# A hybrid attention and convolution layer on one core: an input weight laid out piece by piece, its last piece in another buffer, and one partition sum for two

## The chip, the cores and the metric

One Trainium2 chip, one of its cores. The metric is the device time of one execution in microseconds (us), as a median of repeated runs. "PE" is TensorE, "DVE" VectorE, "ACT" ScalarE, "POOL" GpSimd, "SP" SyncE, which here only issues DMAs.

## The reference, cut to what matters

```python
h = rms_norm(x, pre_norm_gain)
q, k, v, z_a, b_gate, c_gate, u, z_c = split(h @ w_in, 8)
lam = exp(sum(lq1 * lk1)) - exp(sum(lq2 * lk2)) + lambda_init
attn = rms_norm(diff_attention(q, k, v, lam, slopes), subln_gain) * (1 - lambda_init) * silu(z_a)
y = b_gate * causal_conv3(c_gate * u) * silu(z_c)
x = x + rms_norm(concat(attn, y) @ w_out, post_norm_gain)
e = rms_norm(p @ w_ple_proj, ple_norm_gain)
out = x + sigmoid(x @ w_ple_gate) * e
```

x is 1024 positions by 1024 features, p 1024 by 256, all in fp32. The change touches the embedding branch, `e`: the product of p with `w_ple_proj`, and the root mean square over e's 1024 features, of which each position needs one.

## The kernel before, in words

Features lie on the partitions and positions in the free dimension. The 1024 positions are two halves of 512, n = 0 and 1, so a tile is 128 x 512. Every product of two fp32 operands is made of three matmuls in the type fp32r (`mm3`, L99 to L102) from operands split into a high and a low part (`split`, L87 to L93): ACT casts the high part (L89, or L92 with a scale), and DVE or POOL subtracts it from the source (L90, L93).

**Start** (L336 to L361). Nine matmuls on zeros, then `embed` (L322) makes e for half 0 and half 1: eight tiles of 128 features, m = 0 to 7, six matmuls each; each tile is copied by ACT or DVE (L330, L332) and stored to memory, `e_dram` (L333). Its weight `in_w_ple` is loaded in four pieces by `load_ple` (L300): tile 0, tile 1, tiles 2 and 3 with 37 columns of small constants behind them (549 columns), and tiles 4 to 7 (1024 columns). Each piece is split into `wph` and `wpo` (for tiles 0 and 1 by DVE alone, L308, L309; for the others by ACT and DVE, L311). In memory the whole weight is one array of 128 rows by 2085 columns, so that a piece is a band of columns of it. The pieces land in buffers `rawe` of the pool `rawp`, which has three; the fourth piece has to wait for one of them to be read. `load_p` (L313) loads p into `p_raw`, one of the three buffers of the pool `wp` that later hold split weights. `load_x` (L295) loads the 16 tiles of x, `mix`, on the same queue of SP, and splits each into `hT`. `wq` and `wk` (L359, L360) are the first projection's weights, cast by ACT (L89, `w<-raw`).

**Four heads** (L470 to L495). For each head the steps of `PLAN` (L31) are run: `a` softmax of query blocks (`Head.softmax`, L216: PE scores `s`, DVE row maximum and bias at L237, ACT exponential at L241, DVE combination of the two maps at L246 to L249), `g` the values (transposes `tpw` at L260, split by ACT and DVE into `wt`, product `av`), `n` its norm and scale (`scale_values`, L279), `c` tiles of the convolution branch (`Conv`, L410), whose projections `pj` fill PE, `z` the gate, `s` the sums of the embedding.

**Sums of the embedding**, `embed_scale` (L446), run for half 0 in head 0 and half 1 in head 1, behind the values' last instruction (L492). It reads the eight tiles of e again from `e_dram`, ACT squares them (L452) and POOL adds them up (L454), into `mix[7][n]`. `column_sums` (L105) then sums over the partitions: DVE transposes blocks of 32 x 32 (`flip`, L107), reduces them to 16 columns (`part`, L109), and one matmul with a constant, `fold`, (L116) makes the sum, `ms`. `rsqrt` (L95) is one DVE step and a power on POOL (L97, `small_c<-small_c` for the embedding), and L457 halves the result, which is kept in `rs_e`, 16 columns a half, until the last stage needs it. The same `column_sums` serves the heads' norms, with further columns.

**Output** (L498 to L594): the product with `w_out`, its norm, the product with the gate's weight, and the store.

The program's loops only record the work. The order of the instructions on every engine is set afterwards by the scheduler of the tile framework, from its own simulation (`schedule_with_timeline_sim=True`, L628). An engine runs its own list strictly in order. So a change of a few lines can move instructions far from them.

Of the kernel before, what the change touches and what calls it, by code (L numbers as in the profile page):

```python
# [30 lines left out]
PLAN = [  # L31
# [4 lines left out]
]  # L36

# [6 lines left out]
def hybrid_layer(ctx, tc, xT, pT, w_in, lams, w_out, w_ple, w_gate, outT):  # L44
# [11 lines left out]
    tiny = ctx.enter_context(tc.tile_pool(name="tiny", bufs=3))  # L56
    dram = ctx.enter_context(tc.tile_pool(name="dram", bufs=1, space=DRAM))

    small_c = edge.tile([P, 96], F32, name="small_c")
    ps_s = ctx.enter_context(tc.tile_pool(name="ps_s", bufs=3, space=PSUM))  # L60
    ps_a = ctx.enter_context(tc.tile_pool(name="ps_a", bufs=1, space=PSUM))

# [10 lines left out]
    make_identity(nc, ident)  # L73
    fold = const.tile([P, P], F32, name="fold")
    own = small_c[:, 0:4]
    nhalf = small_c[:, 4:20]
    G.memset(nhalf, -0.5)
    sm = small_c[:, 20:57]
    subg = small_c[:, 57:58]
# [22 lines left out]
        T.matmul(out=ps, lhsT=al, rhs=bh, start=False, stop=last)  # L102


    def column_sums(acc, pool, extra=None, tag="flip"):  # L105
        flip = pool.tile([P, HALF], F32, tag=tag, name="flip")
        V.transpose(out=flip, in_=acc)  # L107
        part = tiny.tile([P, 32], F32, tag="part", name="part")
        V.tensor_reduce(out=part[:, 0:16], in_=flip.rearrange("p (f r) -> p f r", r=32), axis=AX.X, op=add)  # L109
        if extra is not None:  # L110
            V.tensor_tensor(out=part[:, 16:32].rearrange("p (t f) -> p t f", t=4),
                            in0=extra.unsqueeze(2).broadcast_to([P, 4, 4]),
                            in1=own.unsqueeze(1).broadcast_to([P, 4, 4]), op=mult)
        n = 16 if extra is None else 32
        ms = bank_t("ms")
        T.matmul(out=ms[:, :n], lhsT=fold, rhs=part[:, :n], start=True, stop=True)  # L116
        return ms
# [37 lines left out]
    with ExitStack() as st:  # L155
# [130 lines left out]
        with ExitStack() as st0:  # L286
            sp = st0.enter_context(tc.tile_pool(name="sp", bufs=1))
            s2 = st0.enter_context(tc.tile_pool(name="s2", bufs=2))

            wph = sp.tile([P, KT, 2, P], F32R, name="wph")  # L290
            wpo = sp.tile([P, KT, 2, P], F32R, name="wpo")

            splits = {}

            def load_x(n, kts=range(KT)):  # L295
                for kt in kts:
                    nc.sync.dma_start(out=mix[kt][n], in_=xT[n, kt])
                    splits[n, kt] = split(hT[n][kt][:, 0], hT[n][kt][:, 1], mix[kt][n], col(C_PRE, kt))

            def load_ple(c, o, queue=nc.sync, constants=0):  # L300
                n = (c.stop - c.start) * 2 * P
                raw = rawp.tile([P, n + constants], F32, tag="raw", name="rawe")
                queue.dma_start(out=raw, in_=w_ple[:, o:o + n + constants])
                if constants:
                    V.tensor_copy(out=sm, in_=raw[:, n:])
                raw = raw[:, :n].rearrange("p (a b c) -> p a b c", b=2, c=P)
                if c.start < 2:
                    V.tensor_copy(out=wph[:, c], in_=raw)  # L308
                    V.tensor_tensor(out=wpo[:, c], in0=raw, in1=wph[:, c].bitcast(F32), op=sub)  # L309
                else:  # L310
                    split(wph[:, c], wpo[:, c], raw)  # L311

            def load_p(n):  # L313
                pth = s2.tile([P, 2, HALF], F32R, tag="pth", name="pth")
                pto = s2.tile([P, 2, HALF], F32R, tag="pto", name="pto")
                raw = p_raw[:, n].bitcast(F32).rearrange("p (k a) b -> p k (a b)", k=2)
                for k in range(2):
                    nc.sync.dma_start(out=raw[:, k], in_=pT[:, n, k])
                    last = split(pth[:, k], pto[:, k], raw[:, k])
                return pth, pto, last  # L320

            def embed(n, p):  # L322
                pth, pto, _ = p
                for m in range(KT):
                    ps = bank_s("ple") if m % 2 else bank_t("ple")
                    for k in range(2):
                        mm3(ps, wph[:, m, k], wpo[:, m, k], pth[:, k], pto[:, k], k == 0, k == 1)
                    e = s2.tile([P, HALF], F32, tag="e", bufs=5, name="e")
                    if m % 2:
                        A.copy(out=e, in_=ps)  # L330
                    else:
                        V.tensor_copy(out=e, in_=ps)  # L332
                    nc.sync.dma_start(out=e_dram[n, m], in_=e)  # L333


            zero = sp.tile([P, HALF], mybir.dt.bfloat16, name="zero")  # L336
            V.memset(zero, 0.0)
            idle = bank_p("idle")
            for _ in range(9):
                T.matmul(out=idle, lhsT=zero[:, :P], rhs=zero, start=True, stop=True)  # L340
            p_raw = wp.tile([P, 2, KT, P], F32R, tag="w", name="p_raw")
            load_ple(slice(0, 1), 0, nc.scalar)
            pt0 = load_p(0)
            load_ple(slice(1, 2), 256)
            load_ple(slice(2, 4), 512, constants=37)
            load_ple(slice(4, 8), 1024 + 37)
            with tc.issue_after(pt0[2][1].ins):
                for g in range(4):
                    V.tensor_reduce(out=fold[:, 32 * g:32 * g + 32], in_=ident.rearrange("p (a b) -> p b a", a=4),
                                    axis=AX.X, op=add)  # L350
                V.tensor_reduce(out=own, in_=ident.rearrange("p (f r) -> p f r", r=32), axis=AX.X, op=add)
            embed(0, pt0)
            V.tensor_scalar(out=subg, in0=sm[:, C_SUB:C_SUB + 1], scalar1=0.4, scalar2=None, op0=mult)
            load_x(0, range(4))
            pt1 = load_p(1)
            load_x(0, range(4, KT))
            embed(1, pt1)
            mixing_weight()
            wq = w_in_tile(0, 0, V)  # L359
            wk = w_in_tile(1, 0, V)  # L360
            load_x(1)  # L361
# [84 lines left out]
        def embed_scale(n):  # L446

            acc = mix[7][n]
            for m in range(KT):
# [2 lines left out]
                A.activation(out=e, in_=e, func=AF.Square)  # L452
                if m:
                    G.tensor_tensor(out=acc, in0=acc, in1=e, op=add)  # L454
            r = rs_e[:, 16 * n:16 * n + 16]
            rsqrt(r, column_sums(acc, ap)[:, :16], D, 1e-6)
            V.tensor_scalar(out=r, in0=r, scalar1=0.5, scalar2=None, op0=mult)  # L457

        convs = [Conv(ct) for ct in range(4)]
        fill = [(part, cv, ev) for cv in convs for part, ev in ((6, cv.ev_u), (5, cv.ev_c), (7, cv.ev_y), (4, cv.ev_b))]  # L460
# [9 lines left out]
        for h in range(H):  # L470
# [5 lines left out]
            for step in PLAN[h]:  # L476
# [8 lines left out]
                elif k == "g":  # L485
                    hd.values(int(v))
                elif k == "n":
                    hd.scale_values(int(v))
                elif k == "c":
                    conv_tiles(int(v))  # L490
                elif k == "s":
                    with tc.issue_after(hd.last.ins):  # L492
                        embed_scale(int(v))
                elif k == "t":
                    conv_tiles(int(v), together=True)  # L495

# [135 lines left out]
```

## Time and profile before

| | us |
|---|---|
| three runs | 639.99, 640.1, 641.1 |
| median | 640.1 |
| the profiled execution | 640.71 |
| its span on the core | 638.9 |
| PE busy | 631.2 (99% of the span) |
| DVE busy | 448.9 (70%) |
| ACT busy | 241.7 (38%) |
| POOL busy | 227.2 (36%) |

The span is the time from the first to the last recorded instruction; 1.8 us of the execution lie outside it. Busy time is the time in which an engine has an instruction in work. A PE that is busy for 99% of the span can only be made to end sooner by taking matmuls away, or by closing the few gaps between them. PE's matmuls overlap: a matmul of 512 columns is listed with about 0.39 us, but the next one starts 0.23 us behind it, so gaps are read from the starts.

### The profile page before, as it was taken

How to read it: one execution, taken by the hardware profiler on the slowest of the kernel's cores; microseconds unless marked ns; L12 is line 12 of the kernel's file. 1: busy time of each engine (PE TensorE's matmuls, PEld its weight loads, DVE VectorE, ACT ScalarE, POOL GpSimd, SP SyncE). 2: the span in 40 equal slices, each digit the busy share in tenths (PEclk: the TensorE clock that was granted, in tenths of full speed). 3: DMA queues.
4: the chain of work that ended last, by engine and by line, in shares of the span. 5: the costliest groups of instructions: out<-in, count | busy, mean ns of one | idle time of the engine just before them, and what ended most of it. 6: DMA issues, size and time to landing. Idle time of an engine off the chain costs nothing.

```text
span 638.9 us, 8065 instructions
## 1 busy us (share of the span) xinstructions
PE 631.2 (99%) x2941; PEld 523.6 (82%) x2941; DVE 448.9 (70%) x825; ACT 241.7 (38%) x441; POOL 227.2 (36%) x114
## 2 busy tenths in 40 slices
PE   8999999999999999999999999999999999999997
PEld 4888888888888888887888888888888888888886
DVE  6978412798786687877886999528992179798342
ACT  5947212433463333542444533223632226313011
POOL 2015100335236545246461142433750087742000
PEclk9999999999999999999999999999999999999999
DMA  8977522310254113342113411100350034124231
GB/s 271 407 285 207 189 98 93 106 34 6 77 153 133 46 34 83 90 144 97 34 42 91 131 34 34 65 35 34 132 230 33 2 98 164 52 83 147 86 113 50
DMA packets 35655, 67.78 MB, mean 106 GB/s; under 512 B 3616, under 2 KB 12448, under 8 KB 35616
## 3 DMA queue, kind: packets, MB, share of 16 engines
q1 hardware_dynamic: 35472, 67.14, 31.9%
q8 instruction: 23, 0.38, 0.2%
q10 hardware_dynamic: 144, 0.13, 0.1%
q14 instruction: 16, 0.13, 0.1%
HBM read 48.38 MB, written 12.58 MB: 95 GB/s over the span
## 4 chain that ended last, share of the span: by engine, by line
PE 92%; DMA 2%; POOL 2%; DVE 1%; ACT 1%; issue 1%; POOLq 0%; ACTq 0%
PE pj L100 15%; PE pj L102 15%; PE pj L101 15%; PE o L102 9%; PE o L100 9%; PE o L101 9%; PE s L233 5%; PE tpw L260 2%; PE v L100 2%; PE v L102 2%; PE v L101 2%; PE av L102 1%; PE av L101 1%; POOL mix L454 1%; PE av L100 1%; PE ple L100 1%
## 5 line engine op out<-in xcount | busy, mean ns | idle before, releaser
L100 PE MATMUL pj<-hT,w 128*128 128x512 f32 x448 | 176.4, 394 | 0.0
L101 PE MATMUL pj<-hT,w 128*128 128x512 f32 x448 | 176.3, 393 | 0.0
L102 PE MATMUL pj<-hT,w 128*128 128x512 f32 x448 | 176.1, 393 | 0.0
L90 POOL TENSOR_TENSOR w<-raw,w 128x1024 fp32r<-128x1024 f32 x41 | 105.7, 2586 | 142.2 <-ACT w L89 142.2
L102 PEld LDWEIGHTS pj<-hT,w 128*128 128x128 f32 x448 | 84.2, 188 | 16.4
L101 PEld LDWEIGHTS pj<-hT,w 128*128 128x128 f32 x448 | 84.2, 188 | 16.2
L100 PEld LDWEIGHTS pj<-hT,w 128*128 128x128 f32 x448 | 84.2, 188 | 16.1
L241 ACT ACTIVATE p<-p,nm 128x128 f32<-128x128 f32 (+7 forms) x64 | 49.4, 773 | 70.4 <-DVE nm L237 60.5
L89 ACT CAST w<-raw 128x1024 fp32r<-128x1024 f32 x44 | 45.8, 1048 | 16.1 <-issue 11.0
L102 PE MATMUL o<-x,w 128*128 128x512 f32 (+1 forms) x136 | 51.3, 377 | 0.0
L100 PE MATMUL o<-x,w 128*128 128x512 f32 (+1 forms) x136 | 51.2, 377 | 0.0
L101 PE MATMUL o<-x,w 128*128 128x512 f32 (+1 forms) x136 | 51.2, 377 | 0.0
L100 PE MATMUL o<-mT,w 128*128 128x512 f32 x128 | 49.8, 389 | 0.0
L101 PE MATMUL o<-mT,w 128*128 128x512 f32 x128 | 49.8, 389 | 0.0
L102 PE MATMUL o<-mT,w 128*128 128x512 f32 x128 | 49.7, 390 | 0.0
L233 PE MATMUL s<-ks,qs 128*128 128x512 f32 (+2 forms) x192 | 47.5, 346 | 0.0
L89 ACT CAST wt<-tpw 128x512 fp32r<-128x512 f32 (+3 forms) x48 | 21.1, 479 | 60.2 <-PE tpw L260 60.2
L90 DVE TENSOR_TENSOR wt<-tpw,wt 128x512 fp32r<-128x512 f32 (+3 forms) x48 | 25.3, 550 | 26.3 <-ACT wt L89 26.1
L237 DVE CUSTOM_DVE_ANT_0 p<-s,bias 128x512 f32<-128x512 f32 (+3 forms) x64 | 34.8, 564 | 9.4 <-PE s L233 5.4
L233 PEld LDWEIGHTS s<-ks,qs 128*128 128x128 f32 x192 | 33.4, 188 | 5.0
L417 POOL TENSOR_TENSOR mix<-mix,R 128x512 f32<-128x512 f32 x8 | 12.3, 1541 | 68.5 <-DVE mix L416 66.4
L249 DVE SCALAR_TENSOR_TENSOR p<-p,rl,p 128x128 f32<-128x128 f32 (+7 forms) x32 | 32.7, 1021 | 0.4
(142 smaller groups left out, 1099.0 us busy)
## 6 DMA issues: line engine op xcount, KB each, us to landing
raw<-in_w_in SPq DMA_DIRECT2D x32, 512.0 KB, 3.8
mix<-in_xT SPq DMA_DIRECT2D x16, 256.0 KB, 5.8
e_dram<-e SPq DMA_DIRECT2D x16, 256.0 KB, 6.0
mix<-e_dram SPq DMA_DIRECT2D x16, 256.0 KB, 3.4
ks<-ks SPq DMA_DIRECT2D x16, 256.0 KB, 3.6
v_dram<-v SPq DMA_DIRECT2D x8, 512.0 KB, 2.6
vs<-v_dram SPq DMA_DIRECT2D x32, 128.0 KB, 2.7
raw<-in_w_out SPq DMA_DIRECT2D x8, 512.0 KB, 3.2
```

The source lines that it names most:

```text
L89: return (A.copy(out=hi, in_=src), (lo_eng or V).tensor_tensor(out=lo, in0=src, in1=hi.bitcast(F32), op=sub))
L90: (lo_eng or V).tensor_tensor(out=lo, in0=src, in1=hi.bitcast(F32), op=sub))
L100: T.matmul(out=ps, lhsT=ah, rhs=bh, start=first, stop=False)
L101: T.matmul(out=ps, lhsT=ah, rhs=bl, start=False, stop=False)
L102: T.matmul(out=ps, lhsT=al, rhs=bh, start=False, stop=last)
L233: T.matmul(out=banks[m][:, :nn], lhsT=s.qs[:, m, qi], rhs=s.ks[:, m, part, c], start=part == 0, stop=part == 1)
L237: V.tensor_tensor_reduce(out=pr[m][:, c0:c0 + n], in0=banks[m][:, :n], in1=s.bias[:, b0:b0 + n], scale=-1.0, scalar=low[m], op0=add, op1=A ...
L241: A.activation(out=pr[m][:, :W], in_=pr[m][:, :W], func=AF.Exp, scale=-1.0, bias=low[m], accum_out=l[:, m:m + 1])
L249: V.scalar_tensor_tensor(out=pr[0][:, :W], in0=pr[1][:, :W], scalar=rl, in1=pr[0][:, :W], op0=mult, op1=add)
L260: T.transpose(out=tp[:, ii * P:(ii + 1) * P], in_=s.ws[ii][:, j * P:(j + 1) * P], identity=ident)
L417: G.tensor_tensor(out=o, in0=o, in1=R[n], op=mult)
L454: G.tensor_tensor(out=acc, in0=acc, in1=e, op=add)
```

## The change

Three edits.

1. The host lays the weight of the embedding out piece by piece: each of its four pieces is one contiguous run of memory, in which the rows of the 128 partitions follow each other.
2. The last piece (tiles 4 to 7) is loaded into the first half of a buffer of the weights' pool `wp`, under the name `w_raw`, instead of into the pool `rawp`.
3. `column_sums` is cut in two. `embed_scale` now ends with the reduced columns (`partial`), written straight into `rs_e`. A new function, `embed_total`, makes the sum over partitions for both halves at once (one matmul of 32 columns, one power, one halving), as the step `e` of head 2, behind `g0`. For that `nhalf`, the exponents of the power, grows from 16 to 32 columns.

```diff
-    ['a0123', 'z', 'v', 'g0', 'a4567', 'g1', 'c1', 'n0', 'c1', 'n1', 'c1'],
+    ['a0123', 'z', 'v', 'g0', 'e', 'a4567', 'g1', 'c1', 'n0', 'c1', 'n1', 'c1'],
...
-    nhalf = small_c[:, 4:20]
+    nhalf = small_c[:, 93:125]
...
+    def partial(part, acc, pool, tag="flip"):
         flip = pool.tile([P, HALF], F32, tag=tag, name="flip")
         V.transpose(out=flip, in_=acc)
+        V.tensor_reduce(out=part, in_=flip.rearrange("p (f r) -> p f r", r=32), axis=AX.X, op=add)
+
+    def column_sums(acc, pool, extra=None, tag="flip"):
         part = tiny.tile([P, 32], F32, tag="part", name="part")
-        V.tensor_reduce(out=part[:, 0:16], in_=flip.rearrange("p (f r) -> p f r", r=32), axis=AX.X, op=add)
+        partial(part[:, 0:16], acc, pool, tag)
...
-                raw = rawp.tile([P, n + constants], F32, tag="raw", name="rawe")
-                queue.dma_start(out=raw, in_=w_ple[:, o:o + n + constants])
+                if c.start == 4:
+                    raw = wp.tile([P, 2, KT, P], F32R, tag="w", name="w_raw")[:, 0].bitcast(F32).rearrange("p a b -> p (a b)")
+                else:
+                    raw = rawp.tile([P, n + constants], F32, tag="raw", name="rawe")
+                queue.dma_start(out=raw, in_=w_ple[P * o:P * (o + n + constants)].rearrange("(p n) -> p n", p=P))
...
-            r = rs_e[:, 16 * n:16 * n + 16]
-            rsqrt(r, column_sums(acc, ap)[:, :16], D, 1e-6)
-            V.tensor_scalar(out=r, in0=r, scalar1=0.5, scalar2=None, op0=mult)
+            partial(rs_e[:, 16 * n:16 * n + 16], acc, ap)
+
+        def embed_total():
+            ms = bank_t("ms")[:, :32]
+            T.matmul(out=ms, lhsT=fold, rhs=rs_e, start=True, stop=True)
+            rsqrt(rs_e, ms, D, 1e-6)
+            V.tensor_scalar(out=rs_e, in0=rs_e, scalar1=0.5, scalar2=None, op0=mult)
```

How the instructions move, at three places. In the rows below a number behind a name tells buffers of one name apart; `mix_k_...` is a tile of the residual (k is the half).

SP's list at the start, before: the loads of p, of the weight's second to fourth piece (128x256, 128x549, 128x1024) and of x.

```order
L318 DMA p_raw<-in_pT 128x512 x2
L303 DMA rawe<-in_w_ple 128x256
L303 DMA rawe<-in_w_ple 128x549
L297 DMA mix_0_110<-in_xT 128x512
L297 DMA mix_0_112<-in_xT 128x512
L297 DMA mix_0_114<-in_xT 128x512
L303 DMA rawe<-in_w_ple 128x1024
L297 DMA mix_0_116<-in_xT 128x512
```

The same place in the changed kernel:

```order
L324 DMA p_raw<-in_pT 128x512 x2
L309 DMA rawe<-in_w_ple 128x256
L309 DMA rawe<-in_w_ple 128x549
L309 DMA w_raw<-in_w_ple 128x1024
L300 DMA mix_0_110<-in_xT 128x512
L300 DMA mix_0_112<-in_xT 128x512
L300 DMA mix_0_114<-in_xT 128x512
L300 DMA mix_0_116<-in_xT 128x512
```

The weight's last piece stands ahead of all tiles of x now; before, three of them were ahead of it.

PE's list at the sum of the embedding's second half, before: `pj` is a projection's bank, `ms` the sum over partitions (16 columns for the embedding, 32 for a head's norm), `tpw` the transposes of the next values. A matmul of plain fp32, such as `ms` or `tpw`, is one row here and two instructions (x2) in the profile.

```order
L102 MATMUL pj<-hT_2_104,w 128x512
L100 MATMUL pj<-hT_3_105,w 128x512
L101 MATMUL pj<-hT_3_105,w 128x512
L116 MATMUL ms<-part,fold 128x16
L260 MATMUL tpw<-ident,p_2493 128x128
L260 MATMUL tpw<-ident,p_2513 128x128
```

The total of both halves in the changed kernel, beside a sum of the head's norm:

```order
L100 MATMUL pj<-hT_0_94,w 128x512
L101 MATMUL pj<-hT_0_94,w 128x512
L102 MATMUL pj<-hT_0_94,w 128x512
L100 MATMUL pj<-hT_1_95,w 128x512
L119 MATMUL ms<-part,fold 128x32
L465 MATMUL ms<-small_c,fold 128x32
L101 MATMUL pj<-hT_1_95,w 128x512
L102 MATMUL pj<-hT_1_95,w 128x512
```

The matmul that read `part` right behind the second half's reduction is gone; in its place one matmul reads `small_c` (of which `rs_e` is a part), further down in head 2.

DVE's list around the transpose of the embedding's second half (`flip<-mix_1_125`), before:

```order
L247 RECIPROCAL rl<-l 128x1
L440 SCALAR_TENSOR_TENSOR mix_0_120<-ty,mix_0_120 128x512
L436 TENSOR_TENSOR y<-pj,R_129 128x512
L107 STREAM_TRANSPOSE flip<-mix_1_125 128x512
L439 SCALAR_TENSOR_TENSOR ty<-ty,y 128x512
L109 TENSOR_REDUCE part<-flip 128x16
L111 TENSOR_TENSOR part<-r_2505,small_c 128x16
```

The same transpose in the changed kernel:

```order
L240 ISA p_2539,nm<-s_2541,bias 128x512
L240 ISA nm 128x1
L240 ISA p_2540,nm<-s_2542,bias 128x512
L240 ISA nm 128x1
L107 STREAM_TRANSPOSE flip<-mix_1_125 128x512
L249 RECIPROCAL r_2493<-l 128x1
L108 TENSOR_REDUCE small_c<-flip 128x16
L215 TENSOR_TENSOR mix_1_115<-pj,R_129 128x512
L114 TENSOR_TENSOR part<-r_2493,small_c 128x16
L250 RECIPROCAL rl<-l 128x1
L240 ISA p_2692,nm<-s_2694,bias 128x384
```

Before, the steps behind it belonged to the convolution branch (`ty`). Now softmax steps of head 2 (L240, which read PE's banks `s`) and the copy out of a projection's bank (L215) stand behind it. The transpose of the first half (`flip<-mix_0_124`) moved in the same way, to between softmax steps and splits `wt` of head 1.

## Rows read from the trace of the kernel before

**Rows 1.** The page: busy time, share of the span and instructions of each engine.

```profile
PE 631.2 (99%) x2941; PEld 523.6 (82%) x2941; DVE 448.9 (70%) x825; ACT 241.7 (38%) x441; POOL 227.2 (36%) x114
```

**Rows 2.** Waits of PE: what waited, for what, us in total, times, longest.

```profile
PE ple L100 <- ACT wph L89: 0.7, 1, 0.7
PE ms L116 <- DVE part L109: 0.7, 1, 0.7
PE ple L100 <- ACT pth L89: 0.4, 1, 0.4
PE ple L101 <- DVE pto L90: 0.2, 1, 0.2
```

**Rows 3.** Timeline of PE, 11.3 to 15.4 us: start, length, instruction [idle before].

```profile
11.53 0.39 PE L102 MATMUL ple<-pth,wpo 128*128 128x512 f32 x1
12.61 0.50 PE L100 MATMUL ple<-pth,wph 128*128 128x512 f32 x1 [0.69 <-ACT wph L89]
12.95 0.39 PE L101 MATMUL ple<-pto,wph 128*128 128x512 f32 x1
...
14.34 0.39 PE L101 MATMUL ple<-pto,wph 128*128 128x512 f32 x1
14.72 0.50 PE L100 MATMUL ple<-pth,wph 128*128 128x512 f32 x1
15.06 0.40 PE L102 MATMUL ple<-pth,wpo 128*128 128x512 f32 x1
```

**Rows 4.** Timeline of PE, 299 to 302 us.

```profile
299.34 0.39 PE L100 MATMUL pj<-hT,w 128*128 128x512 f32 x1
299.57 0.39 PE L101 MATMUL pj<-hT,w 128*128 128x512 f32 x1
300.64 0.40 PE L116 MATMUL ms<-part,fold 128*128 128x16 f32 x2 [0.69 <-DVE part L109]
300.89 0.64 PE L260 MATMUL tpw<-ident,p 128*128 128x128 f32 x4
```

**Rows 5.** The chain of waits, 0 to 20 us: start, length, what.

```profile
6.36 5.13 DMA rawe<-in_w_ple
```

**Rows 6.** Timeline of SP's queue, 0 to 17 us.

```profile
2.58 1.39 SPq L297 DMA_DIRECT2D mix<-in_xT  x3
6.36 0.33 SPq L303 DMA_DIRECT2D rawe<-in_w_ple  x1
```

**Rows 7.** Timeline of ACT, 4 to 24 us.

```profile
7.10 0.62 ACT L89 CAST wph<-rawe 128x512 fp32r<-128x512 f32 x1 [0.46 <-DMA rawe<-in_w_ple]
9.20 1.95 ACT L92 ACTIVATE hT<-mix,small_c 128x512 fp32r<-128x512 f32 x3 [1.47 <-DVE small_c L305]
11.51 1.05 ACT L89 CAST wph<-rawe 128x1024 fp32r<-128x1024 f32 x1 [0.36 <-DMA rawe<-in_w_ple]
...
20.10 2.00 ACT L89 CAST w<-raw 128x1024 fp32r<-128x1024 f32 x2
```

**Rows 8.** Windows: us, busy PE, PEld, DVE, ACT, POOL; PEclk, DMA share, GB/s.

```profile
6.00:7.00 1.00, 0.95 (x3) 0.67 (x4) 0.91 (x3) 0.62 (x1) 0.00 (x0) 1.00 1.04 395
...
11.00:12.00 1.00, 0.92 (x5) 0.41 (x3) 1.00 (x4) 0.64 (x2) 0.00 (x0) 1.00 0.53 123
```

**Rows 9.** Timeline of PE, 22 to 24 us.

```profile
22.58 0.39 PE L100 MATMUL pj<-hT,w 128*128 128x512 f32 x1
```

**Rows 10.** Timeline of DVE, 285 to 303 us.

```profile
289.56 0.69 DVE L439 SCALAR_TENSOR_TENSOR ty<-ty,y 128x512 f32<-128x512 f32 x1 [0.36 <-ACT ty L437]
...
297.12 0.71 DVE L107 STREAM_TRANSPOSE flip<-mix 128x512 f32<-128x512 f32 x1 [3.37 <-POOL mix L454]
297.76 2.24 DVE L439 SCALAR_TENSOR_TENSOR ty<-ty,y 128x512 f32<-128x512 f32 x1
```

**Rows 11.** Timeline of POOL, 272 to 345 us.

```profile
297.05 2.40 POOL L90 TENSOR_TENSOR w<-raw,w 128x1024 fp32r<-128x1024 f32 x1
303.44 2.91 POOL L97 TENSOR_TENSOR small_c<-small_c 128x16 f32<-128x16 f32 x1 [4.00 <-DVE small_c L96]
```

**Rows 12.** Timeline of DVE, 180 to 215 us.

```profile
210.77 0.71 DVE L107 STREAM_TRANSPOSE flip<-mix 128x512 f32<-128x512 f32 x1 [3.43 <-POOL mix L454]
```

**Rows 13.** Windows of 15 us, columns as in rows 8.

```profile
195.00:210.00 15.00, 15.00 (x70) 12.51 (x70) 6.84 (x13) 6.11 (x10) 10.96 (x7) 1.00 0.34 104
...
380.00:395.00 15.00, 15.00 (x73) 12.63 (x72) 14.04 (x32) 6.32 (x12) 5.03 (x3) 1.00 0.11 37
```

**Rows 14.** Timeline of DVE, 303 to 309 us.

```profile
305.67 0.88 DVE L249 SCALAR_TENSOR_TENSOR p<-p,rl,p 128x640 f32<-128x640 f32 x1
306.47 2.37 DVE L457 TENSOR_SCALAR small_c<-small_c 128x16 f32<-128x16 f32 x1
```

More of the change, by code (lines that the diff above doesn't have):

```diff
@@ L57, in hybrid_layer @@
     dram = ctx.enter_context(tc.tile_pool(name="dram", bufs=1, space=DRAM))
-    small_c = edge.tile([P, 96], F32, name="small_c")
+    small_c = edge.tile([P, 224], F32, name="small_c")
     ps_s = ctx.enter_context(tc.tile_pool(name="ps_s", bufs=3, space=PSUM))
@@ L102, in mm3 @@
         T.matmul(out=ps, lhsT=al, rhs=bh, start=False, stop=last)
-    def column_sums(acc, pool, extra=None, tag="flip"):
+    def partial(part, acc, pool, tag="flip"):
         flip = pool.tile([P, HALF], F32, tag=tag, name="flip")
         V.transpose(out=flip, in_=acc)
+        V.tensor_reduce(out=part, in_=flip.rearrange("p (f r) -> p f r", r=32), axis=AX.X, op=add)
+    def column_sums(acc, pool, extra=None, tag="flip"):
         part = tiny.tile([P, 32], F32, tag="part", name="part")
-        V.tensor_reduce(out=part[:, 0:16], in_=flip.rearrange("p (f r) -> p f r", r=32), axis=AX.X, op=add)
+        partial(part[:, 0:16], acc, pool, tag)
         if extra is not None:
@@ L493, in hybrid_layer @@
                         embed_scale(int(v))
+                elif k == "e":
+                    embed_total()
                 elif k == "t":
@@ L621 @@
         "w_out": blocks(w_out),
-        "w_ple": c(np.concatenate([ple[:, :1024], small, ple[:, 1024:]], axis=1)),
+        "w_ple": np.concatenate([ple[:, :256].ravel(), ple[:, 256:512].ravel(),
+                                 np.concatenate([ple[:, 512:1024], small], axis=1).ravel(), ple[:, 1024:].ravel()]),
         "w_gate": blocks(w_ple_gate),
```

## The prediction

> **What bounds the kernel now.** I read the page first: PE is busy for 99% of the span and DVE for 70% [rows 1]. Only fewer matmuls or closed gaps between them can make the end earlier, and anything that opens a gap makes it later by as much. So I took PE's waits next. Behind the first start of the engine there are four of them in the whole span [rows 2]; two, of 0.7 us each, are what the change is aimed at, and the two others (for p's first split, `pth` and `pto`) stay as they are.
>
> The first is at 11.53 us in the embedding's product. Matmuls of 512 columns follow each other every 0.23 us (299.34 to 299.57) [rows 4]. From 11.53 to 12.61 it is 1.08, which loses 0.85; 12.61 to 12.95 and 14.72 to 15.06 are 0.34, which loses 0.11 each; 14.34 to 14.72 is 0.38, which loses 0.15 [rows 3]. Together that is 1.22 us. What it waits for is ACT's cast of the weight's last piece, 11.51 to 12.56 [rows 7], and that waits for the piece itself, issued at 6.36 and in flight for 5.13 us [rows 5]. Why so late is seen on SP: three tiles of x go out from 2.58 to 3.97, then nothing until 6.36 [rows 6]. The piece needed a buffer that was still being read.
>
> The second is at 299.57 us: the next start is at 300.64, 1.07 us instead of 0.23, a loss of 0.84 [rows 4]. `ms` waits for DVE's `part`, whose `flip` DVE could only begin at 297.12, after 3.37 us of idling for POOL's last addition, and a 2.24 us `ty` slipped between the two [rows 10].
>
> **The last piece's buffer and its layout.** The piece is issued right behind the third one, thus at about 2.6, where x begins now [rows 6]. The third piece lands at 7.08, just before its cast at 7.10 [rows 7]. The new one is next in the queue. It is 512 KB; at the 395 GB/s of the stretch from 6 to 7 us [rows 8] that is 1.3 us, so it lands at 8.4. The other bound is a poor stretch of this same stage: from 11 to 12 us, where the old piece was almost alone in flight, 123 GB/s [rows 8]. If half of the piece comes at 395 and half at 123, it takes 0.66 + 2.13 = 2.8 us and lands at 9.9. I take 8.4, because eight neighbouring loads keep the engines filled at that time, and the poor rate is that of a transfer by itself. ACT idles 1.47 us up to 9.20 [rows 7], so the cast (1.05) runs 8.4 to 9.45 instead of 11.51 to 12.56. PE without its gap needs it at 11.53 + 0.23 = 11.76. Even the late bound, 9.9 + 1.05 = 10.95, is in time for that. DVE's split of this piece moves up with the cast, to about 10.5. So the start gains **1.22**, where the x tiles allow it: three of them now come 1.3 us later, and the first of their casts at 9.20 moves to 9.45, but those behind the old cast move up by about 1 us, since it is no longer among them.
>
> Past the start, PE's next need is `w<-raw`, whose two casts run on ACT from 20.10 to 22.10 while the projection that reads them begins at 22.58 [rows 7, 9]. With 1.22 us less it begins at 21.36. ACT has no idle of note from 11.5 on, so its chain must move up too: by the 1.05 of the removed cast, less 0.25 at the front, so the casts end at 21.3 at the latest. The second one is needed only behind three matmuls or more. I cost this at nothing; if ACT's chain does not move, the loss is up to 22.10 - 21.36 = 0.74. SP's other issues (p's second half, x) stand behind a piece that no longer blocks them, and go out earlier. For the layout alone, I count only what is in the 1.3 us.
>
> Here a page speaks against the layout. What the row shows is a piece of 512 KB that takes 5.13 us from issue to landing, with the rate falling to 123 GB/s [rows 5, 8]. The Trainium skill, "DMA: Bandwidth & Descriptors", section "How a descriptor splits into AXI transactions", has it that a descriptor is cut into transactions of 256 bytes, and that a start off that boundary adds one of them. By it a row of 4096 bytes needs 17 instead of 16 at a wrong start: the layout would be worth some 6% of the transfer, an estimate of 0.1 us of the 1.3, and the slow stretch would stay what it is.
>
> **One sum instead of two.** The matmul that waited at 299.57 is gone. Its successor reads `rs_e` some tens of matmuls later, when both reductions lie well behind, as the order shows: the reduction is now between softmax steps early in head 2, and the total is behind `g0`. So the stall of **0.84** goes. One `ms` less is one pair of passes less on PE; from 300.64 to 300.89 it takes 0.25 [rows 4]. Below it is at least half of that. I take **0.2**. A width of 32 instead of 16 columns costs PE nothing I can see, since the heads' norms run 32 with the same functions.
>
> On POOL a power of 16 columns takes 2.91 us [rows 11]. For 32 columns it is between 2.91 and twice that, 5.8. There were two, there is one: POOL's sum changes by between -2.9 and 0. It is not on PE's path: the result is needed in the last stage. What stands behind it on DVE is the halving, which waits for the power; the old one took 2.37 us at 306.47 [rows 14]. What PE needs from DVE behind that are the splits `wt` of the next values, and there DVE waits no longer than before plus 2.9 us. I cost it at nothing, because values follow only some 10 us later; uncovered it would be 2.9.
>
> **What is moved.** `flip`, on which DVE idled 3.43 us in the first half and 3.37 in the second [rows 12, 10], has other work behind it now: softmax steps and a bank's copy, which PE does wait for. Before, the convolution's steps were there, and PE lost only the 0.84. The squares' chain is started by the values of the same head as before, but heads 1 and 2 have their softmax closer behind it. I take it that the idling is mostly gone, for the chain is placed behind more DVE work, and allow 0.2 us for gaps that the new order opens.
>
> **Sum.** 1.22 + 0.84 + 0.2 - 0.2 = 2.1 us less. The profiled execution took 640.7, so 638.6; it lies 0.6 above the median of the runs, 640.1. Against the median it is **638.0**. 0.2%, about what a measurement of this kernel can tell from no change, is 1.28 us: faster ends at 638.8, slower begins at 641.4.
>
> **Rivals.**
>
> *The sums' chain stops DVE in front of softmax* (0.14, slower). DVE's list is in order, and behind `flip` now stand row maxima and a bank's copy. If POOL's last addition comes as late, by DVE's place in its list, as it did before, DVE idles 3.4 us in each half with PE behind it. With all of it on PE that is 3.43 + 3.37 = 6.8 us, so 638.0 + 6.8 = 644.8; with half of it covered by full banks, 641.4. It decides from 3.4 us of new gaps on. I put it at 643. For it: the idling is in the rows, POOL was busy 10.96 of 15 us there [rows 13], and POOL beside DVE makes it slow: the same `ty` step took 0.69 us at 289.56, and 2.24 at 297.76 beside POOL's split from 297.05 on [rows 10, 11]. Against it: in 195 to 210 us DVE was busy for 6.84 of 15, so there is room to move work into; and where DVE had 14.04 of 15, PE still ran 15.00 of 15 [rows 13].
>
> *The power of 32 columns holds DVE* (0.03). In the row, DVE's step with two tensors read went on at 0.88 us for 640 columns at 305.67, within POOL's power from 303.44 to 306.35 [rows 14, 11], so the power did not hold it. Were it held for a whole power of 5.8 us with softmax behind it, the time would be 638.0 + 5.8 = 643.8. The Trainium skill, "SBUF — State Buffer", section "Who interferes with whom", says that a DVE operation with two inputs from SBUF is blocked while GpSimd reads there, for the whole of the instruction. By that rule this is what would happen; the `ty` row agrees with it and the row under the power does not.
>
> *The piece comes late* (0.17). The layout does nothing and the rate is the poor one: landed at 9.9, cast to 10.95, and ACT's other casts move back with it, so `w<-raw` is ready about 0.5 us later than before and PE waits up to 0.74 + 0.2 of its gain away. That leaves 1.22 - 0.9 = 0.3 of the start: 638.9.
>
> *The start's gain is given back* (0.10). The gap closes, but the projection at 22.58 starts where it did, since x or `w<-raw` decide it. Then only 0.84 + 0.2 - 0.2 is left: 639.3.
>
> **How the numbers follow.** My forecast has the rest, 0.56. Faster: it, and a third of the two mild rivals (0.06), 0.62. Same: the rest of these two (0.21) and the mild part of the DVE rival (0.03), 0.24. Slower: 0.14. For 8 in 10 the range reaches below to 636.9 (a whole `ms` and no allowance, 0.25, and other start gaps behind p, up to 0.6) and above to 641.0, past the two mild rivals and into the DVE rival; left out are most of that one, the power, and little below.
>
> **What would show it.** The piece issued by 3 us and landed before 9; no gap of PE over 0.3 us from 7 to 16 us; the first `pj` at about 21.4. No wait of `ms` in PE's list of waits; one power `small_c<-small_c` of 3 to 6 us. PE's busy time lower by about 0.2. Wrong would be: PE waiting for `p` or `s` banks from 195 to 225 or 255 to 290 us, with DVE idle before `flip`; `pj` waiting for `w`; a landing after 9.5.

## The result, and the profile after

| | before | after |
|---|---|---|
| median, us | 640.33 (4 runs) | 648.21 (647.31 to 648.82, 4 runs) |
| ratio, 95% interval | | 1.012 (1.0103 to 1.0138) |
| span of the profiled execution | 638.9 | 646.6 |
| PE busy | 631.2 | 634.3 |

The kernel became slower by 7.9 us, where 2.1 less were forecast. PE's list of waits after the change (what waited, for what, us in total, times, longest) shows at once that the two waits that the change was aimed at are gone, and that others have come (those of `idle`, 1.2 us, and of `ple` for `pto`, 0.2 us, were there before):

```profile
PE pj L100 <- DVE mix L450: 3.1, 1, 3.1
PE s L236 <- DVE nm L240: 1.8, 2, 1.0
PE idle L346 <- DVE zero L343: 1.2, 1, 1.2
PE tpw L263 <- DVE p L252: 0.7, 2, 0.4
PE s L236 <- issue: 0.6, 1, 0.6
PE ple L101 <- DVE pto L90: 0.2, 1, 0.2
```

**The start went as forecast.** ACT's timeline of the changed kernel, to be held against [rows 7], and the first projection's matmul from PE's timeline, against [rows 9]:

```profile
6.89 0.62 ACT L89 CAST wph<-rawe 128x512 fp32r<-128x512 f32 x1 [0.60 <-DMA rawe<-in_w_ple]
8.09 1.05 ACT L89 CAST wph<-w_raw 128x1024 fp32r<-128x1024 f32 x1 [0.58 <-DMA w_raw<-in_w_ple]
9.05 1.95 ACT L92 ACTIVATE hT<-mix,small_c 128x512 fp32r<-128x512 f32 x3
...
18.51 2.00 ACT L89 CAST w<-raw 128x1024 fp32r<-128x1024 f32 x2
```

```profile
21.00 0.39 PE L100 MATMUL pj<-hT,w 128*128 128x512 f32 x1
```

The last piece is there at 8.07 us, 3.4 earlier; the gap at 11.5 us is gone; the first `pj` starts at 21.00 instead of 22.58.

**The loss lies behind 190 us.** Five gaps between PE's starts, at 199.18, 214.29, 286.04, 373.43 and 406.58 us, lose 1.07, 1.15, 0.77, 0.49 and 0.52, together 4.0 us. The first two show the pattern: PE's timeline, then DVE's and POOL's of the same moments (the last two rows of DVE belong to the third and the fourth gap).

```profile
199.18 0.48 PE L236 MATMUL s<-ks,qs 128*128 128x512 f32 x1
200.48 0.73 PE L236 MATMUL s<-ks,qs 128*128 128x512 f32 x2 [0.81 <-DVE nm L240]
...
214.29 0.39 PE L100 MATMUL pj<-hT,w 128*128 128x512 f32 x1
215.67 0.73 PE L236 MATMUL s<-ks,qs 128*128 128x512 f32 x2 [0.99 <-DVE nm L240]
```

```profile
197.19 2.83 DVE L217 SCALAR_TENSOR_TENSOR mix<-tz,mix 128x512 f32<-128x512 f32 x1 [2.33 <-ACT tz L216]
199.94 0.47 DVE L240 CUSTOM_DVE_ANT_0 p<-s,bias,nm 128x256 f32<-128x256 f32 x1
...
211.97 2.90 DVE L286 SCALAR_TENSOR_TENSOR mix<-flipa,small_c,mix 128x512 f32<-128x512 f32 x1
214.80 0.21 DVE L251 SCALAR_TENSOR_TENSOR rl<-rl,l,small_c 128x1 f32<-128x1 f32 x1
214.93 0.68 DVE L240 CUSTOM_DVE_ANT_0 p<-s,bias 128x512 f32<-128x512 f32 x1
...
284.68 1.72 DVE L114 TENSOR_TENSOR part<-r,small_c 128x16 f32<-128x16 f32 x1
...
371.13 2.96 DVE L252 SCALAR_TENSOR_TENSOR p<-p,rl,p 128x512 f32<-128x512 f32 x1
```

```profile
197.08 2.39 POOL L90 TENSOR_TENSOR w<-raw,w 128x1024 fp32r<-128x1024 f32 x1
...
211.94 2.39 POOL L90 TENSOR_TENSOR w<-raw,w 128x1024 fp32r<-128x1024 f32 x1 [4.90 <-ACT w L89]
```

POOL begins to split a weight; 0.11 and 0.03 us later DVE begins a step with two inputs from SBUF. It takes 2.83 and 2.90 us where the same lines take 0.68 and 0.74 at best, and ends about 0.55 us behind POOL's split. Behind it on DVE stands L240, which empties a bank of scores, and PE stands still for that bank. At the other three gaps, too, a DVE step beside a POOL split is the long one: L114 with 1.72 us (0.18 at 369.66), L252 with 2.96 (0.74 at 289.32), and L96 with 2.39 (shown in the last section). Before the change L214 had been caught in the same way in this stretch (198.74, 2.83 us), and PE had projections left to do.

**The largest gap is in the output stage,** 458.37 to 461.88 us, 3.28 us more than 0.23. Timelines of DVE and POOL there:

```profile
451.60 6.87 DVE L90 TENSOR_TENSOR mT<-mix,mT 128x512 fp32r<-128x512 f32 x4
458.40 2.83 DVE L286 SCALAR_TENSOR_TENSOR mix<-flipa,small_c,mix 128x512 f32<-128x512 f32 x1
461.15 0.68 DVE L450 TENSOR_TENSOR mix<-pj,mix 128x512 f32<-128x512 f32 x1
```

```profile
452.29 8.39 POOL L90 TENSOR_TENSOR w<-raw,w 128x1024 fp32r<-128x1024 f32 x3 [2.64 <-ACT w L89]
```

Three weight splits of POOL, one behind the other, let one DVE step pass each: of the four splits `mT` the last two take 2.90 and 2.88 us, then L286 takes 2.83. The four together take 6.87 us, and L450, which frees the bank that PE waits for, comes at 461.15. The gap has a second price. In the next windows (columns as in [rows 8]) PE's granted clock is 0.76 and 0.90 of 2.4 GHz; seven matmuls follow each other at 0.43 instead of 0.23 us, 1.4 us more:

```profile
460.00:465.00 5.00, 3.12 (x9) 2.44 (x10) 4.81 (x7) 2.48 (x5) 0.68 (x1) 0.76 0.84 307
465.00:470.00 5.00, 5.00 (x22) 4.08 (x21) 5.00 (x6) 4.70 (x7) 3.19 (x2) 0.90 0.59 210
```

The account: 4.0 + 3.28 + 1.4 = 8.7 lost; 1.58 at the start and 0.84 at the old wait of `ms` won. That is 6.3 of the 7.7 us by which the span grew. The rest lies in gaps of under 0.3 us each, most of them between 200 and 350 us.

### The profile page after: what moved, and what is told of

It reads as the page before. It is cut to its first block, busy times and chain, and to the rows that moved or that the text cites. A ratio compares the mean times of both kernels' runs of the same rounds, so it can differ in the third digit from the quotient of the medians.

```text
span 646.6 us, 8046 instructions
## 1 busy us (share of the span) xinstructions
PE 634.3 (98%) x2939; PEld 524.4 (81%) x2939; DVE 453.6 (70%) x823; ACT 242.0 (37%) x441; POOL 225.7 (35%) x113
## 4 chain that ended last, share of the span: by engine, by line
PE 70%; DVE 14%; issue 5%; POOL 5%; ACT 2%; DMA 2%; SPq 2%; POOLq 0%; ACTq 0%; DVEq 0%
PE o L102 9%; PE o L100 9%; PE o L101 9%; PE pj L100 9%; PE pj L101 9%; PE pj L102 9%; DVE p L240 3%; PE s L236 2%; PE v L100 2%; PE v L101 2%; PE v L102 2%; DVE p L252 2%; PE tpw L263 2%; SPq L211 2%; POOL rs L97 1%
## 5 line engine op out<-in xcount | busy, mean ns | idle before, releaser
L240 DVE CUSTOM_DVE_ANT_0 p<-s,bias 128x512 f32<-128x512 f32 (+3 forms) x64 | 34.7, 565 | 8.3 <-PE s L236 4.3
L423 POOL TENSOR_TENSOR mix<-mix,R 128x512 f32<-128x512 f32 x8 | 10.8, 1360 | 72.3 <-DVE mix L422 62.3
L547 DVE TENSOR_TENSOR acc<-acc,sqo 128x512 f32<-128x512 f32 x14 | 12.9, 924 | 28.2 <-ACT sqo L546 27.9
```

The lines of the kernel that those rows point to most:

```text
L240: V.tensor_tensor_reduce(out=pr[m][:, c0:c0 + n], in0=banks[m][:, :n], in1=s.bias[:, b0:b0 + n], scale=-1.0, scalar=low[m], op0=add, op1=A ...
L547: V.tensor_tensor(out=accs[n], in0=accs[n], in1=sq, op=add)
```

## The experiments

Two questions: which edit does it, and by what mechanism? Four kernels take the edits apart. The lists show that they can be taken apart: with edits 1 and 2 alone every engine's list differs from before only in the start stage, and with edit 3 alone only from the first head's end on.

### Layout and buffer alone

Against the kernel before:

```diff
-                raw = rawp.tile([P, n + constants], F32, tag="raw", name="rawe")
-                queue.dma_start(out=raw, in_=w_ple[:, o:o + n + constants])
+                if c.start == 4:
+                    raw = wp.tile([P, 2, KT, P], F32R, tag="w", name="w_raw")[:, 0].bitcast(F32).rearrange("p a b -> p (a b)")
+                else:
+                    raw = rawp.tile([P, n + constants], F32, tag="raw", name="rawe")
+                queue.dma_start(out=raw, in_=w_ple[P * o:P * (o + n + constants)].rearrange("(p n) -> p n", p=P))
```

The weight is laid out by the host as in the change; sums, plan and `nhalf` are those of before.

> Edits 1 and 2 alone (layout and buffer), column_sums as before. The lists of all engines are those of before but for the start. Order theory (the loss comes from the new order that edit 3 brings in the middle): the start gains the 1.6 us by which the first pj came earlier in the changed kernel (21.00 instead of 22.58), the stall of ms at 300 us stays, nothing is lost: 638.7 us. Phase theory (an earlier start puts loads and POOL's weight splits beside other DVE steps): new stalls of PE in the middle, 640 to 643 us.

Measured: 639.34 us, ratio 0.9983 (0.9974 to 0.9992). The first `pj` starts at 21.44, the wait of `ms` is the old one, no new wait is in PE's list.

```profile
PE ple L100 <- ACT pth L89: 0.9, 1, 0.9
PE ms L116 <- DVE part L109: 0.8, 1, 0.8
```

So these two edits gain 1.3 us by the medians. The earlier start does not disturb the middle; the phase theory falls.

### One sum for both halves alone

Against the kernel before; `load_ple` and the weight's layout are untouched:

```diff
-            rsqrt(r, column_sums(acc, ap)[:, :16], D, 1e-6)
-            V.tensor_scalar(out=r, in0=r, scalar1=0.5, scalar2=None, op0=mult)
+            partial(rs_e[:, 16 * n:16 * n + 16], acc, ap)
+
+        def embed_total():
...
```

> Edit 3 alone (one sum for both halves, step e), weight and buffer as before. Order theory: the gap at 11.5 us is back, the stalls from 199 to 460 us stay: 648.2 + 1.6 = 649.8 us. Phase theory: the stalls from 199 us on get fewer, 642 to 646 us.

Measured: 650.81 us, ratio 1.0163 (1.0146 to 1.018). All the stalls are there, each 1.7 to 2.3 us later, and the gap at 11.5 us is back. The whole loss comes with edit 3: 10.2 us by the medians. It is 1.0 more than forecast. In this trace the step from a matmul `s` to `tpw` at 282.30 us takes 0.77 (0.40 in the changed kernel), and behind the largest gap twelve matmuls follow each other at 0.43 us instead of seven, which is 1.0 us more; for the medians this is not settled.

### Layout alone, buffer alone

Against the kernel before, the layout alone:

```diff
-                queue.dma_start(out=raw, in_=w_ple[:, o:o + n + constants])
+                queue.dma_start(out=raw, in_=w_ple[P * o:P * (o + n + constants)].rearrange("(p n) -> p n", p=P))
```

and the buffer alone:

```diff
-                raw = rawp.tile([P, n + constants], F32, tag="raw", name="rawe")
+                if c.start == 4:
+                    raw = wp.tile([P, 2, KT, P], F32R, tag="w", name="w_raw")[:, 0].bitcast(F32).rearrange("p a b -> p (a b)")
+                else:
+                    raw = rawp.tile([P, n + constants], F32, tag="raw", name="rawe")
```

> Edit 1 alone (each piece contiguous in memory); every list as before. If the layout matters by itself, the last piece, still issued at about 6.4 us, takes clearly less than 5.1 us to land and the gap of PE at 11.5 us shrinks by that, 639.3 to 639.9 us. If it is only the time of issue that counts: no change, 640.3 us.

> Edit 2 alone (the last piece in a buffer of the weights, a band of columns in memory as before). If the time of issue is all: as with both edits, 638.7 us, the piece landed by 8.5 us. If the layout is needed: the piece lands past 9 us, casts move back, 639 to 640 us.

Measured: layout alone 640.92 us, ratio 1.0008 (1.0 to 1.0017); buffer alone 639.53, ratio 0.9989 (0.998 to 0.9998). The layout does make the transfers shorter: from issue to landing the third piece takes 4.73 us instead of 4.97, the last one 4.25 instead of 5.13. That shortens the gap at 11.5 us as the first branch of the expectation has it, but not the kernel, which was forecast at 639.3 to 639.9. In this trace p's second half lands later (13.88 us instead of 13.54), and PE's gap only changes its place. PE's timeline with the layout alone, and in the chain of waits the transfer that stands behind the second gap:

```profile
11.34 0.39 PE L102 MATMUL ple<-pth,wpo 128*128 128x512 f32 x1
11.95 0.50 PE L100 MATMUL ple<-pth,wph 128*128 128x512 f32 x1 [0.23 <-ACT wph L89]
...
13.69 0.40 PE L101 MATMUL ple<-pto,wph 128*128 128x512 f32 x1
15.06 0.50 PE L100 MATMUL ple<-pth,wph 128*128 128x512 f32 x1 [0.97 <-ACT e L330]
```

```profile
7.25 6.63 DMA p_raw<-in_pT
```

The gap of 0.85 at 11.5 shrinks to 0.38, and 1.14 is lost at 13.69. PE waits there for ACT's copy `e`, which stood behind a cast of p (13.90) that waited for this transfer. The buffer alone has nearly the gain of both. With it the last piece lands at 8.69 us (forecast 8.5), with both edits at 8.19, and the first `pj` starts at 21.72 and 21.44; whether the layout adds something to the time, the intervals of the two do not tell. Most of the gain comes with the time of issue.

### Holding the sum's bank

Why did a sum less move values and softmax? The matmul `ms` takes a bank of the tag `t`, of which there are two, and the transposes `tpw` of the next values use the same two. In the program's order the embedding's sum stood ahead of the next head's values, so `tpw` had to wait for it. Before, they were at 213.16 us, right behind `ms`; in the changed kernel the scheduler puts them earlier, behind the head's own norm (PE's timeline of the changed kernel):

```profile
193.72 0.30 PE L119 MATMUL ms<-part,fold 128*128 128x32 f32 x2
193.86 0.53 PE L263 MATMUL tpw<-ident,p 128*128 128x128 f32 x3
```

The experiment gives the bank its user back, with a matmul that nobody reads, and leaves all else of the change:

```diff
             partial(rs_e[:, 16 * n:16 * n + 16], acc, ap)
+            T.matmul(out=bank_t("held")[:, :16], lhsT=fold, rhs=rs_e[:, 16 * n:16 * n + 16], start=True, stop=True)
```

> The whole change, and behind each of the two reductions a matmul of 16 columns into a bank of the tag t, whose result nobody reads; the transposes tpw use the same two banks, so they stand again where they stood before (head 1: the 934th row of PE's list, as before; in the changed kernel the 857th). Bank theory (the sum's bank had held the values back; without it they run beside POOL's work): the stalls at 199, 214, 373 and 406 us go, the wait for the reduction near 298 us is back, and the stall at 458 us stays, since ACT's list there is that of the changed kernel: about 648.2 - 4.1 = 644.1 us. Rival (the power of 32 columns, the later total and its halving cost the time): no better than 648 us.

Measured: 644.37 us, ratio 1.0061 (1.0048 to 1.0075). The stalls from 199 to 406 us are gone:

```profile
PE pj L100 <- DVE mix L450: 3.1, 1, 3.1
...
PE held L462 <- DVE small_c L108: 0.6, 1, 0.6
```

The step `e` and its power of 32 columns are still in this kernel, so they are not what costs. A matmul into a bank of another tag was not run: that it is the bank, and not just one more matmul there, rests on `tpw` standing where it stood before.

### The output stage's casts

In the output stage ACT's list had changed, among others, at this place. Before:

```order
L89 CAST mT_6_4139<-mix_0_122 128x512
L89 CAST mT_7_4140<-mix_0_124 128x512
L89 CAST w<-raw 128x1024 x3
L437 ACTIVATE ty<-y 128x512
```

In the changed kernel:

```order
L89 CAST mT_6_4132<-mix_0_122 128x512
L89 CAST w<-raw 128x1024 x3
L89 CAST mT_7_4133<-mix_0_124 128x512
L443 ACTIVATE ty<-y 128x512
```

The cast of `mT_7` waits for DVE's L450. As long as it stood ahead of the three weights, POOL's splits could not start before L450 was through. Behind them, it no longer holds them back. DVE's list had moved as well: the copy (L444 before, at 450.25 us) stood ahead of `flipa` and L283; in the changed kernel it is L450 and stands behind `flipa` and L286, one of the long steps above. The experiment leaves this as it is and puts the casts of the first three weights of `w_out` behind that of `mT_7`. It is not quite the old order: the second of these weights was cast well ahead in both kernels (437.5 us before, 440.2 in the changed one). Its lists differ from those of the changed kernel in the output stage alone:

```diff
+        parts = {}
         for n in range(2):
             for kt in range(KT):
-                split(mT[n][kt][:, 0], mT[n][kt][:, 1], mix[kt][n])
+                parts[n, kt] = split(mT[n][kt][:, 0], mT[n][kt][:, 1], mix[kt][n])
+        with tc.issue_after(parts[0, KT - 1][0].ins):
+            for k in range(3):
+                weight(k)
```

> The whole change, and in the output stage ACT's casts of the first three weights put behind its cast of the last mT tile of the first half, as they stood before. Port theory (POOL's three splits of those weights, started by ACT's casts, slow four DVE splits mT ahead of the copy PE waits for): the stall at 458 us (3.3 us, and 1.7 of slower clock behind it) goes, 643.2 us. Rival (DVE is late by itself, since PE was late before): the stall stays, 647 to 648.5 us.

Measured: 643.79 us, ratio 1.0052 (1.0039 to 1.0066). The four splits and the two steps behind them, in DVE's timeline, with POOL's splits below:

```profile
450.32 2.46 DVE L90 TENSOR_TENSOR mT<-mix,mT 128x512 fp32r<-128x512 f32 x4
452.69 0.74 DVE L286 SCALAR_TENSOR_TENSOR mix<-flipa,small_c,mix 128x512 f32<-128x512 f32 x1
453.35 0.68 DVE L450 TENSOR_TENSOR mix<-pj,mix 128x512 f32<-128x512 f32 x1
```

```profile
455.72 10.41 POOL L90 TENSOR_TENSOR w<-raw,w 128x1024 fp32r<-128x1024 f32 x4 [8.14 <-ACT w L89]
```

The same four steps take 2.46 us instead of 6.87. From 458 us on DVE is slow beside POOL here too, and PE, with its operands ready, does not mind: the clock stays at 1.00 from 460 to 470. What is gone is the stall and the slower clock behind it. L450 is still behind L286 on DVE, so its place in the list alone is not what costs.

### The step e in another place

```diff
-    ['a0123', 'z', 'v', 'g0', 'e', 'a4567', 'g1', 'c1', 'n0', 'c1', 'n1', 'c1'],
-    ['a0123', 'z', 'v', 'g0', 'a4567', 'g1', 'c1', 'n0', 'c1', 'n1', 'c3', 't2'],
+    ['a0123', 'z', 'v', 'g0', 'a4567', 'g1', 'c1', 'n0', 'c1', 'n1', 'c1'],
+    ['a0123', 'z', 'v', 'g0', 'a4567', 'g1', 'c1', 'n0', 'c1', 'n1', 'c3', 'e', 't2'],
```

> The whole change with the step e in head 3, ahead of c3, instead of in head 2. The lists stay those of the changed kernel up to 310 us; in the output stage ACT has the last mT tile ahead of the three weights again. Order theory: the stalls from 199 to 406 us stay, that at 458 us goes: 643.2 us. Rival (it is the step e and its power that cost the time): the stalls move to behind the new place and the sum stays at 648 us or falls below 641.

In the kernel that ran, `e` stands behind `c3`, not ahead of it as the expectation says; the order that it speaks of is there. Measured: 644.17 us, ratio 1.0058 (1.0041 to 1.0074). The list of waits has the stalls of `s` (2.3 us) and `tpw` (0.6), and none of `pj`; the gap at 406 us is gone too. ACT casts `mT_7` at 456.5 and the three weights behind it from 457.0 on, as before the change. In the profiled execution (645.28 us) the matmuls from 6.97 to 9.96 us follow each other at 0.43 us, and the first `pj` starts at 22.91 instead of 21.00; the lowest time was 642.98, the forecast 643.2. A move of the small step `e` to another head changed the order in the output stage, and with it 4 us.

### Both repairs together

The bank held and the casts put back, on the whole change (the two diffs above).

> The whole change with both repairs of its order: the reductions' banks held by a matmul of 16 columns each, and ACT's casts of the first three weights of the output behind its cast of the last mT tile of the first half. Bank and port theories together: of the stalls only the wait for the reduction near 298 us is left; 644.4 (banks held alone) - 5.0 (the stall at 458 us with the slower clock behind it) = 639.4 us, thus as with layout and buffer alone (639.3), and the power of 32 columns with its later total costs nothing. Rival (the two repairs overlap, or something else of the third edit costs time): 641 us or more.

Measured: 639.26 us, ratio 0.9986 (0.9975 to 0.9998). PE waits for the zeros at the start and once for the reduction (`held`, 0.7 us), and for nothing else on its list. The whole change, with its order repaired, has the time of layout and buffer alone. So, within these intervals, the new order is all of the loss. Apart from the order, the combined sum neither costs nor gains anything that these runs can tell, since its stall is still there in the held matmul.

### The old stall, without the combined sum

The wait for the second half's reduction came from the step `ty` between transpose and reduction [rows 10]. On DVE the step is put behind the reduction:

```diff
+                with ExitStack() as after:
+                    if s.ct == 1 and n == 1:
+                        after.enter_context(tc.issue_after(embedded[1].ins))
-                V.scalar_tensor_tensor(out=t, in0=t, scalar=1.0, in1=y, op0=add, op1=mult)
+                    V.scalar_tensor_tensor(out=t, in0=t, scalar=1.0, in1=y, op0=add, op1=mult)
```

(`embedded[1]` is the reduction L109 of the second half; edits 1 and 2 are in.)

> Layout and buffer with both sums as before, and on DVE the convolution's step ty put behind the reduction of the embedding's second half (it had slipped between transpose and reduction and took 2.2 us beside POOL's split). The scheduler moves much of heads 2 and 3 after that. Port theory: the wait of ms near 298 us goes (0.97 us there), 638.4 us, if the moved lists bring no other DVE step of two inputs under a POOL split ahead of softmax; each that they bring costs 0.5 to 3 us. Order-blind rival: 638.4 us whatever the rest of the order.

Measured: 638.92 us, ratio 0.998 (0.9971 to 0.9989), the lowest median of all. DVE's timeline:

```profile
295.77 0.71 DVE L109 STREAM_TRANSPOSE flip<-mix 128x512 f32<-128x512 f32 x1 [3.44 <-POOL mix L462]
296.52 0.69 DVE L111 TENSOR_REDUCE part<-flip 128x16 f32<-128x512 f32 x1
297.12 1.00 DVE L113 TENSOR_TENSOR part<-r,small_c 128x16 f32<-128x16 f32 x1
298.04 0.68 DVE L447 SCALAR_TENSOR_TENSOR ty<-ty,y 128x512 f32<-128x512 f32 x1
```

The transpose still waits 3.44 us for POOL, and PE's list has no wait of `ms`. The gap is closed by one step of another order. Against layout and buffer alone the intervals overlap, so the medians do not show that it gains.

## Why the prediction was wrong, point by point

- **Buffer and layout:** right in mechanism. The piece landed at 8.07 (forecast 8.4), the cast ran 8.09 to 9.14, `w<-raw` was cast by 20.5 (forecast 21.3 at the latest). 1.22 was forecast, 1.58 is in the trace of the changed kernel, 1.14 in that of these two edits alone (first `pj` at 21.44), 1.3 in their medians. One reading behind the slower bound was wrong: from 11 to 12 us the old piece was not almost alone in flight, two loads of p and five of x had been issued and had not landed. The layout's part in the gain was not shown: by itself it changes no time. By the rule on descriptors in the Trainium skill, "DMA: Bandwidth & Descriptors", section "How a descriptor splits into AXI transactions", the layout would save some 6% of a transfer, an estimate. Measured from issue to landing are 5% for the third piece and 17% for the last with the layout alone, and 9% and 8% on top of the buffer: the direction agrees, the size varies too much to test the rule.
- **The wait of `ms`:** gone, as forecast, 0.84 us in PE's starts. The 0.2 us for one `ms` less was not seen by itself: PE has two instructions less (2939), but its busy time, forecast to fall by 0.2, rose by 3.1, in part from the slower clock.
- **The power on POOL:** 5.44 us for 32 columns (forecast 2.91 to 5.8), and it held nobody. L252 with 1024 columns took 1.28 us from 316.25 on, inside the power of 316.17 to 321.61. The halving waited 2.04 us for it on DVE with no wait of PE behind it.
- **"What is moved": the step that failed.** It costed the new order at 0.2 us, because the transpose's idling would mostly be gone; the runs show 8.7 us of new gaps and slower clock. As for the idling it was right: DVE did not idle ahead of the first half's transpose at all and 0.74 us ahead of the second's, instead of 3.43 and 3.37 [rows 12, 10]. But the step looked at waits and not at lengths. It took every DVE step at its length of before, while the values, some 19 us earlier now, made DVE's list full, with softmax behind each step: from 195 to 210 us DVE is busy for 11.84 of 15 us now, before for 6.84 [rows 13]. In such a list a step that POOL stretches from 0.7 to 2.9 us can become PE's gap. The row that says so stood in the prediction: `ty`, 0.69 and 2.24 us [rows 10, 11]. It was used as a point for a rival, and not to ask behind which long DVE steps PE would be waiting. The number of long steps is not what changed: between 190 and 450 us, 24 DVE steps were over 0.3 us longer than the shortest of their kind before (33.7 us together), and 23 after (37.3). What changed is what stands behind them.
- **It looked at the middle only.** Over half of the loss, 4.7 of 8.7 us, is in the output stage; putting casts of weights on ACT behind that of `mT_7` takes it away. No rival named that place.
- **The rival on the slower side** (DVE stops in front of softmax, 0.14, 643 us) had the engine and the place of the first part. Its mechanism, waiting for the sums' chain, is not what happened.
- The windows with DVE at 14.04 of 15 us and PE at 15.00 [rows 13] were taken as evidence that PE bears a full DVE. It does where PE has other work for as long as a stretched step lasts. Where scores and their banks alternate, there was none.
- **Two slips in the sums** that did not decide: 0.06 is under a quarter, not a third, of the two mild rivals' 0.27; and the terms given for the lower bound, 0.25 and 0.6, lead from 638.0 to 637.15, not to 636.9.

## What to carry to other kernels

Where a scheduler sets the order, an edit is also what it releases. A sum that was taken out also gave back a PSUM bank which had, unseen, kept the next values in their place, so look at what shares a pool with the thing removed, and read the new lists of all engines to the program's end. Cost a moved list with the lengths that its steps will have beside their new neighbours, and look for the two-input DVE steps under POOL's long ones that stand ahead of something PE waits for; their number alone tells little. An edit that loses by its order can be told from one that loses by its work by putting the order back alone.

## What was not expected of the hardware

- DVE beside POOL. A DVE step of two SBUF inputs that began just behind a weight split of POOL ended about 0.55 us behind it: 0.68 and 0.74 us became 2.83 and 2.90. The Trainium skill, "SBUF — State Buffer", section "Who interferes with whom", has it that the later of the two is blocked until the first is finished. These rows agree, as do four steps `mT` with POOL's splits (6.87 us) and without (2.46); where a split `mT` came first, at 452.17, POOL's split from 452.29 on was the longer one, 2.83 us instead of 2.39. At 371.13 DVE is listed 0.02 us ahead of POOL and is the one that took long; so close an order these rows do not settle. Behind three splits in a row one DVE step passes at each change. POOL's power, which also reads two inputs from SBUF, held no DVE step that began inside it: in none of the traces did one with two SBUF inputs take over 1.3 us there. For the power the rule does not hold as it stands:

```profile
316.25 1.28 DVE L252 SCALAR_TENSOR_TENSOR p<-p,rl,p 128x1024 f32<-128x1024 f32 x1
```

```profile
316.17 5.44 POOL L97 TENSOR_TENSOR small_c<-small_c 128x32 f32<-128x32 f32 x1 [1.13 <-DVE small_c L96]
```

  The other way round it did wait: the power at 406.16, begun 0.16 us behind a DVE step L252 of 1.27 us, took 3.87 us instead of 2.90. A DVE step of a single input was caught by a weight split too, which the same section allows for `tensor_scalar` in its two-port modes; in which mode it ran no row shows:

```profile
403.70 2.39 DVE L96 TENSOR_SCALAR rs<-rs 128x16 f32<-128x16 f32 x1
```

  This one, of 16 columns, stood beside a POOL split from 403.67 to 406.05; without one it takes 0.17. The halving of 2.37 us in [rows 14] has the same neighbour, a split from 306.33 to 308.81.
- PE's clock. After the gap at 458 us, in which PE had nothing in work for 3.1 us, the granted clock fell to 0.76 over 460 to 465 us, of a full 2.4 GHz; matmuls at 0.43 us instead of 0.23 are those of about the 1.2 GHz level. From 407.33 us to the gap no two starts of PE had been more than 0.32 us apart. That made 3.3 us of waiting cost 4.7. The price is not fixed: the same gap of 3.5 us between starts was followed by seven such matmuls here and by twelve with edit 3 alone. The gaps of 1.1 to 1.2 us at 199 and 214 had no such sequel; the granted clock is 1.00 over 195 to 220 us.
